# The head of a two-layer encoder trunk: first bias distances in the setup, two weight quarters in split form, the rope table behind the last split

## The chip, the cores and the metric

The kernel runs on one core of one Trainium2 chip. Its time is the device time in microseconds (us) of one execution, from first to last. Engines are named as the profile names them: PE is the matrix engine (TensorE) and PEld its weight loads, DVE is VectorE, ACT is ScalarE, POOL is GpSimd, SP is SyncE, which here only issues DMAs.

## The reference

The reference is a trunk of two layers over 256 tokens of width 2048, in float32. What matters for the change is the start of the first layer:

```
cond = silu(c)
for l in range(2):
    mod = cond @ w_ada[l] + b_ada[l]              # 2048 -> 6 * 2048
    sh_a, sc_a, g_a, sh_m, sc_m, g_m = split(mod, 6)
    h = rmsnorm(x) * (1 + sc_a) + sh_a
    proj = h @ w_in[l]                            # 2048 -> 3904 columns: dq, dk, dv, cq, ckv, kr
    ...  # differential attention with a bias by position distance,
    ...  # latent attention with rope on part of q and k
    x = x + g_a * (concat(out_a, out_b) @ w_o[l])
    h = rmsnorm(x) * (1 + sc_m) + sh_m
    x = x + g_m * (relu(h @ w_mlp_in[l])**2 @ w_mlp_out[l])
return rmsnorm(x, final_norm_g)
```

The bias of the differential attention is a table of 32 buckets by 4 heads, looked up by the bucket of the difference of two positions. Rope turns pairs of features by angles position times frequency, so it needs a table of cosines and sines.

## The kernel before, in words

Activations lie with features on the 128 partitions and the 256 tokens along the free dimension. The 2048 features are 16 k tiles, taken as eight pairs p = 0 to 7.

**Two forms of a weight.** A weight block is multiplied in one of two forms.

- Whole form: the float32 block is loaded straight into tiles of the tags `hi` and `lo` (`by_k_weights`, line 225) and multiplied with the float32 activation (line 244). One such product of 128 x 128 weights with 256 tokens shows up as two PE instructions in the trace.
- Split form: the block is loaded into a tile of the tag `raw` (line 156). ACT rounds each half of it into a `hi` tile (line 144), DVE takes the difference into a `lo` tile (line 145), and the product is three PE instructions (lines 180 to 182: hi times h's hi, hi times h's lo, lo times h's hi).

The tags `hi` and `lo` have four buffers each, and the tag `raw` has five, shared with the tiles of w_ada:

```
hi = self.wp.tile([P, half], F32R, tag="hi", name=self.name("hi"), bufs=4)
lo = self.wp.tile([P, half], F32R, tag="lo", name=self.name("lo"), bufs=4)
raw = self.wp.tile([P, width], F32, tag="raw", name=self.name("raw"), bufs=5)
```

**The head.** `setup` loads x, the condition and constants, and prepares the bias (`bias_setup`). `first_norm_then_by_k` then walks over the eight pairs. For each pair, four tiles of w_ada (1 MB each, `ada_load`, line 306) are multiplied with the condition and summed on DVE (`ada_sums`, line 322); this gives shift and scale of the pair's two k tiles (lines 334 and 336). DVE normalizes the pair (line 603), ACT applies scale and shift (line 614) and writes h's hi part (line 620), DVE writes h's lo part (line 626). PE multiplies the pair with the first 1536 columns (`w_a`, 12 tiles of 128 columns, two blocks). Pairs 0 to 5 (`WHOLE = 6`) are in whole form, pairs 6 and 7 in split form.

**What is filled in.** `FILL = "0|1|2|3||||rlm"` hangs small jobs behind the pairs: behind pairs 0 to 3 one part each of the bias, behind pair 7 the rope table (`rope_setup`), the lambdas and their end. A bias part needs distances (`bias_rel`: five DVE instructions, lines 472, 475 and 478), marks of the buckets (ACT line 489 and 494, DVE line 497) and 16 PE instructions (lines 507 and 508).

**The second columns.** `EARLY = {4: (0, 1), 6: (2,)}` names quarters of a second block of 512 columns (`w_d`, the rest of q and a part of k; a quarter is four k tiles, 1 MB). Quarters 0 and 1 are multiplied behind pair 4, quarter 2 behind pair 6, quarter 3 after the pairs. In the kernel before, quarters 0 to 2 are in whole form, since the float32 activations `whole` are there, and quarter 3 is in split form.

**Order.** The program is written in one sequence; a scheduler puts the instructions of each engine into an order of its own, by their place in the sequence and by when their data and buffers are there. `behind(a, b)` is a hint that a is issued after b on its engine. Each engine then runs its queue in order, and SP issues the DMAs in order.

Of the kernel before, what the change touches and what calls it, by code (L numbers as in the profile page):

```python
# [9 lines left out]
F32 = mybir.dt.float32  # L10
# [3 lines left out]
ALU = mybir.AluOpType  # L14
# [3 lines left out]
T = 256  # L18
# [40 lines left out]
def two_pi_parts():  # L59
    parts, rest = [], 2.0 * math.pi  # L60
    for _ in range(6):
        e = math.floor(math.log2(rest))
        q = 2.0 ** (e - 5)
        part = math.floor(rest / q) * q
        parts.append(part)
        rest -= part
    parts.append(rest)
    return parts
# [34 lines left out]
class Trunk:  # L103
# [31 lines left out]
    def weights(self, src, width=2048):  # L135
        nc = self.nc
        raw = self.raw(src, width)
        out = []
        half = width // 2
        for i in range(2):  # L140
            v = raw[:, i * half : (i + 1) * half]
            hi = self.wp.tile([P, half], F32R, tag="hi", name=self.name("hi"), bufs=4)
            lo = self.wp.tile([P, half], F32R, tag="lo", name=self.name("lo"), bufs=4)
            nc.scalar.activation(hi, v, AF.Copy)  # L144
            ins = nc.vector.tensor_tensor(lo, v, hi.bitcast(F32), ALU.subtract)  # L145
            out.append((hi, lo))
        self.ada_sums(self.hold or ins)
        self.credit += self.rate
        while self.credit >= 1.0 and self.ada_todo:
            self.credit -= 1.0  # L150
            self.ada_load()
        return out
# [200 lines left out]
    def setup(self):  # L353
        nc, io, cp = self.nc, self.io, self.cp
        self.ada_plan()
        self.cond = cp.tile([P, D], F32, name="cond")
        ck = cp.tile([P, NK], F32, name="ck")
        nc.sync.dma_start(ck, io["ck"])
        self.vec = cp.tile([P, NVEC], F32, name="vec")
        nc.sync.dma_start(self.vec, io["vec"])  # L360
        self.eps = cp.tile([P, 1], F32, name="eps")
        nc.gpsimd.memset(self.eps, EPS)
        self.K = cp.tile([P, NCONST], F32, name="K")
        nc.sync.dma_start(self.K, io["consts"])
        self.pos = cp.tile([P, T + 8], I32, name="pos")
        nc.sync.dma_start(self.pos, io["pos"])
        self.ones = cp.tile([P, P], F32, name="ones")
        nc.gpsimd.memset(self.ones, 1.0)
        self.ident = cp.tile([P, P], F32, name="ident")
        make_identity(nc, self.ident)  # L370
        xt = [[None, None], [None, None]]
        for h in range(2):
            for t in range(2):
                xt[t][h] = self.wp.tile([P, D // 2], F32, tag=("hi", "lo")[h], name=self.name("xt"), bufs=4)
                nc.sync.dma_start(xt[t][h], io["x"][t, :, D // 2 * h : D // 2 * h + D // 2])
        nc.scalar.activation(ck, ck, AF.Silu)
        nc.scalar.activation(self.s("root", 1), ck[:, :1], AF.Sqrt, bias=self.eps, scale=0.0)
        for j in range(4):
            c = slice(512 * j, 512 * j + 512)
            ps = self.bank("pc").rearrange("p a b -> p (a b)")  # L380
            for i in range(4):
                col = ck[:, 4 * j + i : 4 * j + i + 1].broadcast_to([P, P])
                nc.tensor.transpose(ps[:, i * P : i * P + P], col, self.ident)
            if j % 2:
                cond_dve = nc.vector.tensor_copy(self.cond[:, c], ps)
            else:
                cond_act = nc.scalar.activation(self.cond[:, c], ps, AF.Copy)
        self.bias_setup(cond_dve, cond_act)
        self.x = cp.tile([P, NK, T], F32, name="x")
        tot = self.sp.tile([P, 2, 2], F32, tag="s22", name="xsq")  # L390
        for h in range(2):
            for t in range(2):
                junk = self.bias[:, 2 * t : 2 * t + 2].rearrange("p a b c -> p (a b c)")
                ins = nc.scalar.activation(junk, xt[t][h], AF.Square, accum_out=tot[:, h, t : t + 1])
                self.behind(ins, cond_act)

        def turn(n, after=None):
            h, p = n // 4, n % 4
            ps = self.bank("px")
            for i in range(2):  # L400
                c = (2 * p + i) * P
                for t in range(2):
                    nc.tensor.transpose(ps[:, i, t * P : (t + 1) * P], xt[t][h][:, c : c + P], self.ident)
            k = 8 * h + 2 * p
            ins = nc.scalar.activation(self.x[:, k : k + 2], ps, AF.Copy)
            if after is not None:
                self.behind(ins, after)

        return tot, turn
# [108 lines left out]
    def rope_setup(self):  # L518
        nc, K, pos = self.nc, self.K, self.pos
        tl = lambda s: self.tp.tile([P, T], F32, tag="t", name=self.name(s))  # L520
        ang, k, r = tl("ang"), tl("kk"), tl("rr")
        self.behind(nc.vector.tensor_copy(ang, pos[:, :T]), self.last_mod)
        nc.vector.tensor_scalar(ang, ang, K[:, C_FREQ : C_FREQ + 1], None, ALU.mult)
        magic = 1.5 * 2.0**23
        nc.vector.tensor_scalar(k, ang, 1.0 / (2.0 * math.pi), magic, ALU.mult, ALU.add)
        nc.vector.tensor_scalar(k, k, -magic, None, ALU.add)
        src = ang
        for part in two_pi_parts():
            nc.vector.scalar_tensor_tensor(r, k, -part, src, ALU.mult, ALU.add)
            src = r  # L530
        pi = 3.1415925
        nc.vector.tensor_scalar(r, r, -pi, pi, ALU.max, ALU.min)
        self.cos = self.cp.tile([P, T], F32, name="cos")
        self.sin = self.cp.tile([P, T], F32, name="sin")
        c = tl("cc")
        nc.vector.tensor_scalar(c, r, -1.0, None, ALU.mult)
        nc.vector.tensor_tensor(c, c, r, ALU.max)
        nc.vector.tensor_scalar(c, c, -1.0, math.pi / 2.0, ALU.mult, ALU.add)
        nc.scalar.activation(self.sin, r, AF.Sin)
        nc.scalar.activation(self.cos, c, AF.Sin)  # L540
        nc.vector.tensor_scalar(self.sin, self.sin, K[:, C_SGN : C_SGN + 1], None, ALU.mult)
# [139 lines left out]
    def first_norm_then_by_k(self, acc, src, n, fill, early):  # L681
# [8 lines left out]
        ins = self.nc.scalar.activation(r, ps, AF.Copy)  # L690
# [3 lines left out]
        h, whole, made = [], [], []  # L694
# [14 lines left out]
        def first():  # L709

            nc = self.nc
            w = [[self.wp.tile([P, 6 * P], F32, tag=tag, name=self.name("w"), bufs=4) for tag in ("hi", "lo")]
                 for _ in range(2)]

            def load(i):
                self.ada_load()
                self.ada_load()
                for b in range(2):
                    nc.sync.dma_start(w[b][i], src[0, b, :, 6 * P * i : 6 * P * i + 6 * P])

            def second():
                load(1)
                self.ada_sums()

            load(0)
            self.ada_sums()
            self.behind(self.sums[0], sum_x)
            self.behind(self.sums[1], root)
            t = self.normed(r, 0, True)
            norm = self.last_norm  # L730
            new, lows, ins = self.scaled(t, 0, sh, sc, whole, second)
            self.rel = [self.bias_rel(a, norm) for a in range(2)]
            h.extend(new)
            made.append(ins)
            return lows, [(x, 6 * P) for x in w]

        lows, blocks = first()
        for p in range(8):
            if p:
# [33 lines left out]
    def layer(self, l, acc):  # L773
        nc, io = self.nc, self.io
# [5 lines left out]
        def next_by_k(kqs):  # L780
            def f(h, whole=()):
                if not later:
                    later.extend(self.open_banks(2))
                for kq in kqs:
                    f32 = whole if 4 * kq + 4 <= len(whole) else None
                    blocks = self.by_k_weights([io["w_d"][l, kq]], 4, f32)
                    self.by_k(later, blocks, h, 4 * kq, NK, 4, f32)
            return f
# [17 lines left out]
        kk, qn, kn, qr, vm, a, at, v, o = [], [], [], [], [], [], [], [], []  # L806
# [413 lines left out]
```

## Time and profile before

| | us |
|---|---|
| median of 3 runs | 2212.98 (2211.97 to 2214.62) |
| the profiled execution | 2212.55 |
| its span, first to last instruction | 2210.8 |
| PE busy | 2180.0 |
| DVE busy | 1625.5 |
| ACT busy | 1136.4 |
| bytes read | 581.28 MB, 264 GB/s over the span |

The busy time of PE is a share of the span, but matmuls are pipelined and their ends are modelled, so the pace of PE is better read from the starts of successive instructions. The head of the program, in which the change lies, is roughly the first 145 us of the span.

### The profile page before, as it was taken

To read this page: it belongs to the slowest core of one execution; us is meant where nothing else is said; L and a number is where in the kernel's file an instruction comes from. 1 tells how busy PE (TensorE), PEld (TensorE's weight loads), DVE (VectorE), ACT (ScalarE), POOL (GpSimd) and SP (SyncE) were. 2 spreads that over 40 slices of the span, in tenths; PEclk is the share of its full clock that TensorE was granted. 3 is DMA by queue.
4 is the path that set the end of the run, shared out by engine and by line. 5 is a ranking of instruction groups with operands and counts; after the bars stand their busy time and mean duration, and the time that the engine had idled before them with its cause. 6 is when DMAs were issued, how large, how long until landed. Compare 5 with 4: busy or idle time off the path is not lost.

```text
span 2210.8 us, 32403 instructions
## 1 busy us (share of the span) xinstructions
PE 2180.0 (99%) x13010; PEld 1948.1 (88%) x13010; DVE 1625.5 (74%) x2273; ACT 1136.4 (51%) x1691; POOL 1.9 (0%) x10
## 2 busy tenths in 40 slices
PE   7999999999999999999999999999999999999998
PEld 6899888998888888888889988988888888888887
DVE  7899779988878888887886876788655555555555
ACT  6555663465464355355444565546535534534553
POOL 0000000000000000000000000000000000000000
PEclk9999999999999999999999999999999999999999
DMA  9988778888878888888867666677655555555552
GB/s 379 415 348 311 265 269 327 316 328 325 322 305 321 305 323 310 318 324 304 316 218 265 248 229 228 236 263 253 240 189 193 184 189 192 188 183 192 188 189 95
DMA packets 85255, 585.49 MB, mean 265 GB/s; under 512 B 9584, under 2 KB 9968, under 8 KB 19440
## 3 DMA queue, kind: packets, MB, share of 16 engines
q1 hardware_dynamic: 85104, 583.42, 71.1%
q8 instruction: 102, 1.67, 0.3%
q14 instruction: 49, 0.40, 0.0%
HBM read 581.28 MB, written 2.10 MB: 264 GB/s over the span
## 4 chain that ended last, share of the span: by engine, by line
PE 93%; DVE 4%; DMA 2%; ACT 1%; issue 1%; SPq 0%; DVEq 0%; ACTq 0%
PE ps L201 43%; PE ps L204 22%; PE pk L244 3%; PE pk L182 2%; PE pk L181 2%; PE pk L180 2%; PE pk L258 2%; DVE ada L322 2%; PE pv L269 1%; PE pv L270 1%; PE pv L271 1%; DMA ada<-in_w_ada 1%; DVE lo L145 1%; PE pk L260 1%; PE ps L181 1%; PE ps L180 1%
## 5 line engine op out<-in xcount | busy, mean ns | idle before, releaser
L145 DVE TENSOR_TENSOR lo<-raw,hi 128x1024 fp32r<-128x1024 f32 (+1 forms) x714 | 843.0, 1194 | 466.9 <-issue 189.0
L144 ACT ACTIVATE hi<-raw 128x1024 fp32r<-128x1024 f32 (+1 forms) x714 | 731.3, 1035 | 690.6 <-PE ps L201 312.5
L201 PE MATMUL ps<-hid,hi 128*128 128x512 f32 x2048 | 477.5, 390 | 0.0
L322 DVE SCALAR_TENSOR_TENSOR ada<-ada,cond 128x2048 f32<-128x2048 f32 x192 | 438.6, 2286 | 13.6 <-DMA ada<-in_w_ada 13.5
L201 PEld LDWEIGHTS ps<-hid,hi 128*128 128x128 f32 x2048 | 379.7, 188 | 78.1 <-DVE hid L174 1.4
L201 PE MATMUL ps<-h,hi 128*128 128x512 f32 x1856 | 431.7, 390 | 0.0
L201 PEld LDWEIGHTS ps<-h,hi 128*128 128x128 f32 x1856 | 344.7, 188 | 69.2
L204 PEld LDWEIGHTS ps<-hid,lo 128*128 128x128 f32 x2048 | 254.2, 192 | 5.0
L204 PE MATMUL ps<-hid,lo 128*128 128x256 f32 x2048 | 255.7, 283 | 0.0
L204 PEld LDWEIGHTS ps<-h,lo 128*128 128x128 f32 x1856 | 230.3, 192 | 4.5
L204 PE MATMUL ps<-h,lo 128*128 128x256 f32 x1856 | 231.7, 283 | 0.0
L973 DVE SCALAR_TENSOR_TENSOR x<-ps,mod,x 128x256 f32<-128x256 f32 x272 | 124.6, 479 | 6.8 <-PE ps L204 6.6
L979 ACT ACTIVATE sum<-ps 128x256 f32<-128x256 f32 x110 | 42.2, 383 | 115.3 <-PE ps L204 115.1
L182 PE MATMUL pk<-h,lo 128*128 128x256 f32 x320 | 90.4, 283 | 0.0
L181 PE MATMUL pk<-h,hi 128*128 128x256 f32 x320 | 90.4, 283 | 0.0
L180 PE MATMUL pk<-h,hi 128*128 128x256 f32 x320 | 90.1, 285 | 0.0
L244 PE MATMUL pk<-hf,w 128*128 128x256 f32 x384 | 83.9, 379 | 0.0
L244 PEld LDWEIGHTS pk<-hf,w 128*128 128x128 f32 x384 | 72.6, 190 | 10.1 <-ACT hf L614 0.4
L174 DVE TENSOR_TENSOR hid<-relu,hid 128x256 fp32r<-128x256 f32 x128 | 48.3, 422 | 44.8 <-ACT hid L173 44.8
L182 PEld LDWEIGHTS pk<-h,lo 128*128 128x128 f32 x320 | 61.4, 192 | 0.2 <-DVE lo L145 0.2
L181 PEld LDWEIGHTS pk<-h,hi 128*128 128x128 f32 x320 | 61.4, 192 | 0.1
L180 PEld LDWEIGHTS pk<-h,hi 128*128 128x128 f32 x320 | 61.0, 192 | 0.1
(229 smaller groups left out, 2387.0 us busy)
## 6 DMA issues: line engine op xcount, KB each, us to landing
raw<-in_w_m SPq DMA_DIRECT2D x238, 1024.0 KB, 4.8
ada<-in_w_ada SPq DMA_DIRECT2D x192, 1024.0 KB, 4.9
raw<-in_w_ob SPq DMA_DIRECT2D x24, 1024.0 KB, 5.5
raw<-in_w_m SPq DMA_DIRECT2D x24, 768.0 KB, 5.7
raw<-in_w_dv SPq DMA_DIRECT2D x16, 1024.0 KB, 4.8
raw<-in_w_t SPq DMA_DIRECT2D x12, 1024.0 KB, 4.8
w<-in_w_a SPq DMA_DIRECT2D x24, 384.0 KB, 13.8
raw<-in_w_a SPq DMA_DIRECT2D x12, 768.0 KB, 5.4
```

Source lines behind the costliest of these rows:

```text
L144: nc.scalar.activation(hi, v, AF.Copy)
L145: ins = nc.vector.tensor_tensor(lo, v, hi.bitcast(F32), ALU.subtract)
L174: self.nc.vector.tensor_tensor(lo, val[:, i], hi.bitcast(F32), ALU.subtract)
L180: mm(ps, hi, x[0], start=first, stop=False, skip_group_check=shared)
L181: mm(ps, hi, x[1], start=False, stop=False, skip_group_check=shared)
L182: mm(ps, lo, x[0], start=False, stop=last, skip_group_check=shared)
L201: mm(ps.rearrange("p a b -> p (a b)"), part(w, k, 0), x[2], start=k == 0, stop=False)
L204: mm(ps[:, 0], part(w, k, 1), x[0], start=False, stop=k == nk - 1)
L244: self.nc.tensor.matmul(ps, v, whole[k], start=first, stop=last, skip_group_check=True)
L258: mm(ps.rearrange("p a b -> p (a b)"), part(j, 0), both, start=k == 0, stop=False)
L322: ins = nc.vector.scalar_tensor_tensor(w, w, 1.0, self.cond, ALU.mult, ALU.mult, accum_out=acc[:, i : i + 1])
L973: self.nc.vector.scalar_tensor_tensor(x, ps[i][:, j], g[:, m + i : m + i + 1], x, ALU.mult, ALU.add)
```

## The change

Three steps are changed.

- The distances of bias part 0 are computed at the end of `bias_setup`, where nothing orders them behind other work; before, `first` computed those of parts 0 and 1 behind the first normalization.
- Of the quarters of the second columns that are done early, only quarter 2 stays in whole form. Quarters 0 and 1 go to the split form: one DMA of 1 MB each into a `raw` tile, two roundings on ACT and two differences on DVE each, and 48 PE instructions in the place of 32.
- The first instruction of the rope table is ordered behind the last split (`last_lo`) that was written before it, which is that of pair 7; before, it was ordered behind the last shift and scale (`last_mod`).

```
@@ weights
-            ins = nc.vector.tensor_tensor(lo, v, hi.bitcast(F32), ALU.subtract)
+            ins = self.last_lo = nc.vector.tensor_tensor(lo, v, hi.bitcast(F32), ALU.subtract)
@@ setup
         self.bias_setup(cond_dve, cond_act)
+        self.rel = [self.bias_rel(0)]
@@ rope_setup
-        self.behind(nc.vector.tensor_copy(ang, pos[:, :T]), self.last_mod)
+        self.behind(nc.vector.tensor_copy(ang, pos[:, :T]), self.last_lo)
@@ first_norm_then_by_k, first
-            self.rel = [self.bias_rel(a, norm) for a in range(2)]
+            self.rel.append(self.bias_rel(1, norm))
@@ layer, next_by_k
-                    f32 = whole if 4 * kq + 4 <= len(whole) else None
+                    f32 = whole if kq == 2 else None
                     blocks = self.by_k_weights([io["w_d"][l, kq]], 4, f32)
                     self.by_k(later, blocks, h, 4 * kq, NK, 4, f32)
```

## The prediction

> **What bounds the kernel now.** I read the page first, then a table of stretches of 10 us over the head (four of them are shown), then the timelines of PE, DVE, ACT and SP around the three places of the change, then single DMAs with their time to landing. The page's head and its chain of waits:
>
> ```profile
> span 2210.8 us, 32403 instructions
> PE 93%; DVE 4%; DMA 2%; ACT 1%; issue 1%; SPq 0%; DVEq 0%; ACTq 0%
> ```
>
> The chain is PE almost to the end. So a shift of PE at the end of the head goes through to the end of the kernel. The head, by stretches (busy time of PE, PEld, DVE, ACT, POOL, then granted clock, DMA share, GB/s):
>
> ```profile
> 30.00:40.00 10.00, 6.70 (x25) 5.31 (x24) 9.96 (x13) 5.09 (x9) 0.00 (x0) 0.83 1.02 411
> 90.00:100.00 10.00, 10.00 (x48) 8.81 (x47) 6.01 (x8) 1.71 (x4) 0.00 (x0) 1.00 1.02 404
> 120.00:130.00 10.00, 10.00 (x76) 9.71 (x75) 9.86 (x14) 0.68 (x2) 0.00 (x0) 1.00 1.02 411
> 140.00:150.00 10.00, 10.00 (x87) 10.00 (x85) 7.99 (x9) 9.12 (x15) 0.00 (x0) 1.00 0.87 312
> ```
>
> From 90 to 130 us two things are full at once: PE without a gap, and the DMA queue (share 1.02, 404 to 411 GB/s, which is some 2.5 us for 1 MB). DVE and ACT have room from 90 to 100. In the stretch from 140 the DMA is no longer full.
>
> **Part 1, the first distances.**
>
> ```profile
> 13.29 0.16 DVE L688 TENSOR_TENSOR rms<-xsq 128x2 f32<-128x2 f32 x1 [1.97 <-ACT bias L394]
> 26.71 1.27 DVE L475 SCALAR_TENSOR_TENSOR rel<-fl,rt 128x256 f32<-128x256 f32 x3
> 27.90 0.42 DVE L478 TENSOR_SCALAR rel<-rel 128x512 f32<-128x512 f32 x1
> 43.41 2.29 DVE L322 SCALAR_TENSOR_TENSOR ada<-ada,cond 128x2048 f32<-128x2048 f32 x1 [2.14 <-DMA ada<-in_w_ada]
> ```
>
> Two of the three L475 (0.4 us each) and one L478 (0.42) leave the stretch at 27 us: 1.2 us of DVE there. DVE is back in step at 43.41, where it stands 2.14 us for a w_ada tile; that tile lands by a DMA queue that is full, so DVE being earlier before it buys nothing. In the setup the five instructions (about 1.9 us) lie in the wait of 1.97 us in front of 13.29. If that cover were gone, they would delay the root by up to 1.9 us, and the 2.14 us would swallow it. I take 0, with bounds of -0.3 and +0.3.
>
> **Part 2, the two quarters.** PE around the pairs 4 to 7:
>
> ```profile
> 70.31 10.52 PE L244 MATMUL pk<-hf,w 128*128 128x256 f32 x48
> 84.31 34.69 PE L244 MATMUL pk<-hf,w 128*128 128x256 f32 x160
> 118.65 0.70 PE L180 MATMUL pk<-h,hi 128*128 128x256 f32 x3
> 119.55 0.28 PE L181 MATMUL pk<-h,hi 128*128 128x256 f32 x1
> 119.67 0.28 PE L182 MATMUL pk<-h,lo 128*128 128x256 f32 x1
> 134.19 0.47 PE L180 MATMUL pk<-h,hi 128*128 128x256 f32 x1
> ...
> 134.77 0.39 PE L182 MATMUL pk<-h,lo 128*128 128x256 f32 x1
> 134.99 0.28 PE L180 MATMUL pk<-h,hi 128*128 128x256 f32 x1
> ```
>
> The 160 instructions are pair 4 (48), the two quarters (64) and pair 5 (48), at 34.69 / 160 = 0.217 us each. The split form starts one each 0.12 us. So the quarters take 64 x 0.217 = 13.9 us now and 96 x 0.12 = 11.5 us after: 2.35 us less PE.
>
> Against it stands when the first split is ready. PE is through with pair 4 at 84.31 + 48 x 0.217 = 94.7.
>
> ```profile
> 80.62 0.33 SPq L225 DMA_DIRECT2D w<-in_w_d  x1
> w<-in_w_d SPq DMA_DIRECT2D x1, 512.0 KB, 14.4
> L144 ACT ACTIVATE hi<-raw 128x1024 fp32r<-128x1024 f32 x642 | 671.5, 1057 | 616.0 <-PE ps L201 301.1 <-DMA raw<-in_w_m 87.2 <-DVE lo L145 81.6
> L145 DVE TENSOR_TENSOR lo<-raw,hi 128x1024 fp32r<-128x1024 f32 x642 | 774.9, 1220 | 454.8 <-issue 188.4 <-PE ps L204 172.6 <-ACT hi L144 93.5
> 95.02 1.09 ACT L614 ACTIVATE hf<-hf,mod,mod 128x256 f32<-128x256 f32 x2 [7.61 <-DVE mod L334]
> 96.02 0.71 ACT L620 ACTIVATE h<-hf 128x256 fp32r<-128x256 f32 x2
> 103.97 2.29 DVE L322 SCALAR_TENSOR_TENSOR ada<-ada,cond 128x2048 f32<-128x2048 f32 x1 [7.72 <-DMA ada<-in_w_ada]
> ```
>
> The second half of quarter 0 lands now at 80.62 + 14.4 = 95.0. As one DMA of 1 MB at the same place of a full queue, the quarter lands as a whole then. ACT's rounding takes 1.06 and DVE's difference 1.22. If ACT takes the rounding at once, the first split is ready at 95.0 + 1.06 + 1.22 = 97.3; behind the two L614 that become ready at the same moment (1.09) at 98.4; behind the two L620 also (0.71) at 99.1. PE starts two instructions of a product before it needs the lo tile (0.24). So PE stands 2.4, 3.4 or 4.1 us where it stood not at all. I take the middle, 3.4, since L614 comes earlier in the written sequence. The rest of the chain holds: half a quarter is 24 x 0.12 = 2.9 us of PE, and one rounding plus one difference is 2.3 us; DVE has its hole of 7.72 us in front of 103.97 for the four differences (4.9), ACT its idle stretch. Part 2 is then 3.4 - 2.35 = +1.05 us, with ends of 0 and +1.8.
>
> The standing itself may have a price of its own. At 33 us PE stood 3.3 us:
>
> ```profile
> 36.55 0.77 PE L507 MATMUL pb<-oh,lsch 128*128 128x512 f32 x1 [3.30 <-DVE oh L497]
> 37.11 0.63 PE L508 MATMUL pb<-oh,lscl 128*128 128x512 f32 x1
> 38.81 0.63 PE L508 MATMUL pb<-oh,lscl 128*128 128x512 f32 x1
> 40.00 0.40 PE L508 MATMUL pb<-oh,lscl 128*128 128x512 f32 x1
> 40.24 0.39 PE L507 MATMUL pb<-oh,lsch 128*128 128x512 f32 x1
> ```
>
> Behind it the starts are 1.70 / 4 = 0.43 us apart (37.11 to 38.81) instead of 0.24 (40.00 to 40.24); six of them lost some 1.2 us, and the stretch from 30 to 40 shows a clock of 0.83. [...]
>
> **Part 3, the rope table.** For pair 7 the starts 134.19 to 134.99 take 0.80 us for a product that takes 0.36 elsewhere: 0.44 lost.
>
> ```profile
> 129.21 0.29 DVE L522 CAST ang<-pos 128x256 f32<-128x256 int32 x1
> 131.58 2.26 DVE L529 SCALAR_TENSOR_TENSOR rr<-kk,rr 128x256 f32<-128x256 f32 x5
> 133.76 1.82 DVE L145 TENSOR_TENSOR lo<-raw,hi 128x768 fp32r<-128x768 f32 x2
> 138.46 1.04 ACT L144 ACTIVATE hi<-raw 128x1024 fp32r<-128x1024 f32 x1
> ```
>
> Rope starts at 129.21 on DVE, in front of pair 7's first difference at 133.76. With rope behind the differences the 0.44 us go. The price: rope's 15 steps on DVE, of 0.29 us (129.21) to 0.45 (five in 2.26), make 4.4 to 6.8 us, say 5.7, that now end later, and its sine and cosine on ACT may stand in front of quarter 3's rounding, at 138.46 now. PE needs that when it is through with pair 7's 24 products: 134.19 + 24 x 0.36 = 142.8. Pair 7's last difference can start when quarter 2 leaves PE at 134.19, and takes 0.9 (two in 1.82), so rope runs from 135.1 to 140.8; with sine and cosine in front (some 1.2 from the rows of ACT, as long as two L614) and then a rounding and a difference (2.3), PE would stand up to 1.5 us; if the rounding goes first, 0. I take +0.4, near the end at which the rounding goes first, since its data is there earlier. Part 3 is 0, between -0.4 and +1.
>
> **The sum.** 0 + 1.05 + 0 = +1.0 us on the profiled execution's 2212.55 (its span of 2210.8 and 1.75 around it), 2213.6. The median of the runs, 2212.98, is 0.43 higher, so the forecast for a median is 2214.0. This counts as no change: a measurement of this kernel can tell about 0.2%, which is 4.4 us.
>
> **The rivals.**
>
> *Held loads (slower).* Quarters 0 and 1 now fill eight hi and lo tiles instead of four, which is all there are.
>
> ```profile
> 87.09 8.10 SPq L225 DMA_DIRECT2D w<-in_w_a  x4
> 95.28 2.68 SPq L306 DMA_DIRECT2D ada<-in_w_ada  x4
> raw<-in_w_t SPq DMA_DIRECT2D x1, 1024.0 KB, 5.1
> 113.37 0.84 ACT L144 ACTIVATE hi<-raw 128x768 fp32r<-128x768 f32 x1 [16.64 <-issue]
> 115.99 0.75 DVE L626 TENSOR_TENSOR h<-hf,h 128x256 fp32r<-128x256 f32 x2
> ```
>
> Now pair 5's four loads leave from 87.09 to 95 as PE frees pair 4's tiles. If the quarters get these tiles first, pair 5's loads wait until PE is through with half of quarter 0: 98.1 + 2.9 = 101.0. SP issues in order, so the w_ada tiles of pair 6 (95.28) wait behind them. The queue runs dry when quarter 1 has landed (97.5) and moves again 5.1 - 2.5 = 2.6 us after the issue, at 103.6: a hole of 6.1 us in a queue that is full to 140. Pair 6's first raw tile, rounded at 113.37 now, comes at 119.5; from rounding to the pair's lo parts it is 3.4 us (113.37 to 116.74), so pair 6 starts near 122.9 instead of 118.65, +4.2, and the later loads, up to 6.1 late, add about 1: +5, 2218.0. It decides as soon as the hole is over 3 us. For it: tiles are short, and SP is in order. Against it: pair 5's loads need no data first, so they can be given the tiles that pair 3 freed by 70.31 + 10.4 = 80.7, before quarter 0 has landed; then they leave even earlier than now.
>
> *Clock halved behind the stand.* The forecast plus 1.2 us, 2215.2, if the stand is long enough.
>
> *No stand (faster).* If quarter 0 were loaded ahead of the last w_ada tile of pair 5, 2.5 us sooner, the stand is about 1 or none. Then 2.35 and 0.44 us come in, less what pair 6 asks back: PE would be there at 116.3, and its lo parts end at 116.74. That is -2.3 us, 2210.7. Against it: the written sequence puts the w_ada tiles first.
>
> *A difference behind a sum.* The last difference of quarter 1 is needed near 106.7. If DVE's order puts the sum of 103.97 (and the next) in front of it, it ends at 107.5 or 110: +0.8 to +3.3, 2214.8 to 2217.3. Then the change does only a part of what it says.
>
> **How the numbers follow.** Forecast 0.45; clock 0.15; held loads 0.22; no stand 0.10; difference behind a sum 0.08. Time: the forecast's 2214.0. The low end 2210.0 takes in "no stand" with 0.7 us of the spread of the runs; the high end 2218.5 takes in "held loads" at +5 with 0.5 for the clock. Outside lie held loads together with the halved clock, and an order of the later program that comes out otherwise. Slower by over 0.2% (above 2217.4): most of held loads, a part of the difference behind a sum, and the clock on top of either, 0.30. Faster by over 0.2% needs more than any term gives; I keep 0.10 for "no stand" with a better order behind it. Within: 0.60.
>
> **What would show it.** Right: 96 instructions of L180 to L182 between pair 4 and pair 5, 0.12 us apart, with PE waiting 2.4 to 4.1 us on L145 in front of them; pair 5's loads issued before 95; DMA share still 1.0 from 100 to 130; rope's first instruction behind pair 7's last L145 and no 0.44 us at pair 7. Held loads: a hole in the DMA share around 100 and pair 5's loads at 101 or later. Clock: starts 0.24 us apart and a granted clock under 1 behind the stand. The prediction is wrong if PE does not stand in front of the quarters, or if pair 7 starts more than 3 us from 135.

## The result and the profile after

The changed kernel takes 2216.4 us (median; 2213.8 to 2220.9), the kernel before, run beside it, took 2211.9 (2210.3 to 2216.4). The ratio is 1.002, with an interval of 1.0013 to 1.0027: slower by some 4.5 us, about the size of the 0.2% that the prediction called no change. The profiled execution took 2215.82 us against 2212.55, +3.3. Span and chain of waits on the page of the changed kernel:

```profile
span 2214.0 us, 32466 instructions
PE 88%; DVE 7%; DMA 4%; issue 1%; ACT 0%; SPq 0%; DVEq 0%; ACTq 0%
```

DVE and DMA have grown from 6% to 11% of the chain. The stretches (columns as above: busy time of five engines, granted clock, DMA share, GB/s) show where:

```profile
90.00:100.00 10.00, 6.68 (x34) 5.54 (x33) 8.34 (x12) 4.97 (x8) 0.00 (x0) 0.99 0.98 407
100.00:110.00 10.00, 10.00 (x74) 10.00 (x73) 6.92 (x8) 0.53 (x1) 0.00 (x0) 0.84 0.55 202
```

The second of them in the kernel before:

```profile
100.00:110.00 10.00, 10.00 (x49) 8.79 (x48) 5.81 (x6) 0.00 (x0) 0.00 (x0) 1.00 1.01 421
```

Two things are new. PE stands for 3.3 us between 90 and 100 and runs at a granted clock of 0.84 in the next 10 us. And in those same 10 us the DMA moves half of what it moved before (202 against 421 GB/s). The timeline of PE gives the first:

```profile
84.41 10.52 PE L244 MATMUL pk<-hf,w 128*128 128x256 f32 x48
97.73 0.39 PE L180 MATMUL pk<-h,hi 128*128 128x256 f32 x1 [2.80 <-ACT hi L144]
98.99 0.39 PE L182 MATMUL pk<-h,lo 128*128 128x256 f32 x1 [0.52 <-DVE lo L145]
100.23 0.42 PE L180 MATMUL pk<-h,hi 128*128 128x256 f32 x1
100.44 0.41 PE L181 MATMUL pk<-h,hi 128*128 128x256 f32 x1
100.66 0.41 PE L182 MATMUL pk<-h,lo 128*128 128x256 f32 x1
111.61 10.53 PE L244 MATMUL pk<-hf,w 128*128 128x256 f32 x48
121.78 0.47 PE L180 MATMUL pk<-h,hi 128*128 128x256 f32 x1
131.24 7.17 PE L244 MATMUL pk<-hf,w 128*128 128x256 f32 x32 [0.48 <-DMA w<-in_w_d]
146.89 0.28 PE L424 MATMUL pl<-vec,ones 128*128 128x4 f32 x2
```

Pair 4 ends at 94.93. The stand is 2.80 us at the first product and 0.52 at the first `lo`. Behind it instructions start 0.21 us apart (100.23, 100.44, 100.66) instead of 0.12. Pair 6, at 118.65 before, starts at 121.78: +3.1. The last row is the first product of the lambdas' sums. In the kernel before it is this one, 3.6 us earlier:

```profile
143.27 0.28 PE L423 MATMUL pl<-vec,ones 128*128 128x4 f32 x2
```

That row is the measure used from here on, "the sums". Behind it each kernel of this study needs another 2066.6 to 2069.7 us, so the sums leave up to 3 us of the whole time open. ACT and DVE around the stand:

```profile
95.03 1.09 ACT L615 ACTIVATE hf<-hf,mod,mod 128x256 f32<-128x256 f32 x2 [7.55 <-DVE mod L334]
96.02 0.71 ACT L621 ACTIVATE h<-hf 128x256 fp32r<-128x256 f32 x2
96.64 3.89 ACT L144 ACTIVATE hi<-raw 128x1024 fp32r<-128x1024 f32 x4
97.71 4.63 DVE L145 TENSOR_TENSOR lo<-raw,hi 128x1024 fp32r<-128x1024 f32 x4 [1.45 <-ACT hi L144]
112.68 2.29 DVE L322 SCALAR_TENSOR_TENSOR ada<-ada,cond 128x2048 f32<-128x2048 f32 x1 [5.72 <-DMA ada<-in_w_ada]
116.39 2.29 DVE L322 SCALAR_TENSOR_TENSOR ada<-ada,cond 128x2048 f32<-128x2048 f32 x1 [1.41 <-DMA ada<-in_w_ada]
```

ACT takes the roundings last, behind both pairs of activations. And DVE stands 5.72 us at 112.68 and 1.41 at 116.39 for w_ada tiles that pair 6 needs. Why they are late is in SP's queue (start, duration of the group, what it issues):

```profile
82.90 4.81 SPq L156 DMA_DIRECT2D raw<-in_w_d  x2
89.86 2.81 SPq L306 DMA_DIRECT2D ada<-in_w_ada  x2
102.81 3.92 SPq L225 DMA_DIRECT2D w<-in_w_a  x4
106.78 0.90 SPq L306 DMA_DIRECT2D ada<-in_w_ada  x2
```

Pair 5's four loads leave at 102.81, where they left at 87.09 before. They wait for `hi` and `lo` tiles, which the split quarters hold until PE is through with half of quarter 0 (its 24th instruction starts at 102.58); two w_ada tiles wait behind them in order.

### The profile page after: what moved, and what is told of

Same layout as the page of the kernel before. It is cut to its first block, busy times and chain, and to the rows that moved or that the text cites. A ratio compares the mean times of both kernels' runs of the same rounds, so it can differ in the third digit from the quotient of the medians.

```text
span 2214.0 us, 32466 instructions
## 1 busy us (share of the span) xinstructions
PE 2180.5 (98%) x13042; PEld 1950.1 (88%) x13042; DVE 1629.7 (74%) x2277; ACT 1140.0 (51%) x1695; POOL 1.9 (0%) x10
## 4 chain that ended last, share of the span: by engine, by line
PE 88%; DVE 7%; DMA 4%; issue 1%; ACT 0%; SPq 0%; DVEq 0%; ACTq 0%
PE ps L201 42%; PE ps L204 22%; DMA ada<-in_w_ada 3%; DVE ada L322 3%; PE pk L182 3%; PE pk L180 3%; PE pk L181 3%; DVE lo L145 2%; PE pk L258 2%; PE pv L269 1%; PE pv L270 1%; PE pv L271 1%; PE pk L260 1%; PE pk L244 1%; PE pw L600 1%
## 5 line engine op out<-in xcount | busy, mean ns | idle before, releaser
L180 PE MATMUL pk<-h,hi 128*128 128x256 f32 x352 | 100.2, 287 | 2.8 <-ACT hi L144 2.8
L182 PE MATMUL pk<-h,lo 128*128 128x256 f32 x352 | 100.0, 285 | 0.5 <-DVE lo L145 0.5
L181 PE MATMUL pk<-h,hi 128*128 128x256 f32 x352 | 100.1, 285 | 0.0
L180 PEld LDWEIGHTS pk<-h,hi 128*128 128x128 f32 x352 | 67.9, 194 | 3.3 <-ACT hi L144 3.2
L244 PE MATMUL pk<-hf,w 128*128 128x256 f32 x320 | 70.3, 379 | 0.5 <-DMA w<-in_w_d 0.5
L182 PEld LDWEIGHTS pk<-h,lo 128*128 128x128 f32 x352 | 68.3, 194 | 0.7 <-DVE lo L145 0.7
L244 PEld LDWEIGHTS pk<-hf,w 128*128 128x128 f32 x320 | 60.5, 190 | 9.0 <-DMA w<-in_w_d 0.7
L181 PEld LDWEIGHTS pk<-h,hi 128*128 128x128 f32 x352 | 68.3, 194 | 0.1
```

The costliest lines, as they stand in the source:

```text
L180: mm(ps, hi, x[0], start=first, stop=False, skip_group_check=shared)
L181: mm(ps, hi, x[1], start=False, stop=False, skip_group_check=shared)
L182: mm(ps, lo, x[0], start=False, stop=last, skip_group_check=shared)
L244: self.nc.tensor.matmul(ps, v, whole[k], start=first, stop=last, skip_group_check=True)
```

## The experiments

Three theories were to be told apart. A: PE's own loss, the stand and the slow stretch behind it, makes the time. B: the held loads make it, through a hole in a DMA queue that has no time to spare. C: the split form is dear wherever it lies. All thirteen kernels first; "pair 4" and "the sums" are the starts on PE in the profiled execution, GB/s is the mean of six stretches of 10 us from 80 to 140, ratios are against the kernel before, run beside each of them with medians of 2211.5 to 2212.1 us.

| kernel | ratio (interval) | pair 4 | the sums | GB/s 80-140 |
|---|---|---|---|---|
| before | 1 | 84.3 | 143.3 | 413 |
| the change | 1.002 (1.0013 to 1.0027) | 84.4 | 146.9 | 381 |
| split alone | 1.0023 (1.0013 to 1.0032) | 84.4 | 147.8 | 381 |
| distances and rope alone | 1.0007 (0.9999 to 1.0016) | 84.9 | 143.6 | 413 |
| rope alone | 1.0003 (0.9994 to 1.0012) | 83.8 | 142.5 | 417 |
| stand filled | 1.0021 (1.0012 to 1.003) | 83.9 | 146.1 | 388 |
| quarters loaded early | 1.0027 (1.0017 to 1.0036) | 85.8 | 148.0 | 376 |
| one quarter split | 1.001 (1.0001 to 1.0019) | 84.8 | 146.6 | 399 |
| whole, twice the buffers | 1.0028 (1.0017 to 1.0038) | 84.5 | 147.6 | 379 |
| split behind pair 5 | 1.001 (1.0001 to 1.0019) | 84.2 | 143.4 | 403 |
| whole behind pair 5 | 1.0021 (1.0012 to 1.003) | 84.5 | 145.5 | 402 |
| split, lows in raw ring | 1.0016 (1.0007 to 1.0025) | 85.7 | 145.2 | 392 |
| the same, loaded early | 1.0008 (0.9999 to 1.0017) | 84.6 | 144.9 | 398 |
| behind pair 5, raw ring | 1.0027 (1.0017 to 1.0037) | 84.3 | 148.1 | 371 |

By and large the last two columns go together: the fewer bytes are moved from 80 to 140, the later the sums. Between the change and before, 32 GB/s over 60 us are 1.9 MB, which take 4.6 us at 413 GB/s. That alone does not show which is the cause, since a late PE also frees tiles late and so holds loads back. And each profile is a single execution, from 2.4 us below (split, lows in raw ring) to 1.8 us above (behind pair 5, raw ring) the median of its kernel: a difference of a us at the sums needs the medians beside it.

**The parts of the change.** The split alone:

```
 (kernel before)
-    f32 = whole if 4 * kq + 4 <= len(whole) else None
+    f32 = whole if kq == 2 else None
```

> The kernel before with the second step alone: quarters 0 and 1 of the second columns in split form, distances and rope as before. Theory A (the loss is the quarters: PE stands from 94.9 until the first split is ready, and runs slowly behind the stand) and theory B (the loss is the loads of pair 5 and 6 that are held for tiles) both expect all of the loss here: pair 5 starts near 111.6 as in the changed kernel instead of 108.6, and the time is 3 to 5 us over the kernel before, with up to 0.5 more than in the changed kernel if the move of rope is worth something. A rival (the move of the distances or of rope costs the time) expects the time of the kernel before.

2217.26 us, ratio 1.0023: 5.7 us over the kernel before, a little more than the 3 to 5 expected. The loss is the split's. Its profile shows the same stand (3.11 us), the same slow products and the same hole as the whole change, and pair 5 at 111.54.

Distances and rope alone (the change with that line as it was):

> The changed kernel with quarters 0 and 1 back in whole form: first distances in the setup and rope behind pair 7's splits remain. Theories A and B expect the time of the kernel before, within 0.5 us, or up to 0.4 us less, since pair 7 then starts without the 0.44 us that its first product lost at 134.19. The rival that one of these two moves costs the time expects 2 to 4 us more than the kernel before.

2213.22 us, 1.6 us over the kernel before where at most 0.5 was expected, but with an interval that holds 1. The sums are 0.4 us later in a run whose pair 4 started 0.6 later.

The rope alone (kernel before):

```
-    self.behind(nc.vector.tensor_copy(ang, pos[:, :T]), self.last_mod)
+    self.behind(nc.vector.tensor_copy(ang, pos[:, :T]), self.last_lo)
```

> The kernel before with the rope's tables moved behind the last split and nothing else. By the prediction: 0.4 us gained at pair 7's first product, and at most as much lost behind it; the layer's sums start at 142.9 to 143.5 us (143.3 before), the time is 2211.2 to 2212.2 us. Rival, the rope moved is what makes up the 0.9 us by which the change with the split alone is later at the sums (147.8 us) than the whole change (146.9): then its place is worth 0.9 us here too, the sums start near 142.4 us and the time is 2211 us or under; and a second rival, that it costs: its sine falls among the roundings of quarter 3 or the first key block, the sums start at 143.6 us or later, as they do in the kernel with distances and rope moved.

2212.84 us, a little over the expected 2211.2 to 2212.2, and no difference that the interval shows. From pair 4 to the sums it is 58.7 us, in both runs with whole quarters and the rope moved, against 59.0 before: about 0.25 us gained in the head, where 0.44 were expected. The sums at 142.5 look like the first rival, but 0.5 us of that stood at pair 4 already, and the time did not follow. Of the 0.9 us between the split alone and the whole change the rope's place is only a part (see "Open" below).

**PE's stand, filled.** Twenty products of 128 x 128 between pair 4 and quarter 0, whose result is overwritten, keep PE busy where it stood:

```
 (the change; next_by_k, ahead of quarter 0)
+    if l == 0 and kq == 0:
+        for _ in range(20):
+            ins = nc.tensor.matmul(later[1][:, 1, :P], self.ident, whole[9][:, :P], start=True, stop=True, ...)
```

> The changed kernel, with 20 idle matmuls of 128 x 128 put on PE between pair 4 and quarter 0 (they write a bank that the quarter then starts anew), so that PE is busy while it waits for the first split. Theory A with its clock part: the products of quarter 0 start 0.36 us apart at once instead of 0.64 from 99.7 to 103.3, and pair 5 starts 1.6 us earlier, near 110.0. If the stand and the clock alone set the time, the kernel is 1.6 us faster than the changed one (about 2214.8 against 2216.4). Theory B: pair 6 has its data no earlier than about 121.6 (its lo parts in the changed kernel), so it starts within 0.3 us of 121.8 as before and the time is that of the changed kernel. If the slow stretch behind the stand is not due to the stand, the spacing of 0.64 us stays.

2216.31 us, as the change, where A alone expected 2214.8. PE's timeline and two of its stretches:

```profile
94.29 4.63 PE L790 MATMUL pk<-hf,ident 128*128 128x128 f32 x40
98.67 0.36 PE L180 MATMUL pk<-h,hi 128*128 128x256 f32 x1
98.87 0.28 PE L181 MATMUL pk<-h,hi 128*128 128x256 f32 x1
100.00:110.00 10.00, 10.00 (x85) 10.00 (x85) 6.68 (x7) 0.28 (x1) 0.00 (x0) 1.00 0.74 247
120.00:130.00 10.00, 9.42 (x76) 9.14 (x74) 9.96 (x12) 2.07 (x3) 0.00 (x0) 1.00 1.01 407
```

The clock is 1.00 from 100 to 110 and 85 instructions start there instead of 74, so the slow stretch is a consequence of the stand. Pair 5 starts at 110.27, as A expected (110.0), and pair 6 at 120.44, which is 1.1 us sooner than B allowed (121.5). One reason is that the two are linked: tiles come free as PE moves on, so pair 5's loads leave at 101.70 instead of 102.81. But the sums come only 0.8 us sooner: PE, earlier now, waits for data between 120 and 130 (1.0 us for quarter 2). A alone does not make the time.

**The stand taken away.** The raw loads of quarters 0 and 1 are issued ahead of pair 5's w_ada tiles:

```
 (the change; first_norm_then_by_k)
+    if p == 4:
+        self.ahead = [self.raw(self.io["w_d"][0, kq], 2048) for kq in (0, 1)]
     lows = ready(p + 1)
 (by_k_weights and weights then take these tiles instead of loading their own)
```

> The changed kernel, with the two 1 MB loads of quarters 0 and 1 issued ahead of the four w_ada tiles of pair 5 instead of behind them. Theory A alone: the first split is ready before 94.9, PE does not stand, the quarters take 11.5 us, pair 5 starts near 106.4 and everything behind comes 2.3 us earlier than in the kernel before: about 2209.6. Theory B: pair 5's four loads still wait for tiles that quarter 0 holds until PE is through with its halves (97.8 and 100.7), the DMA queue has a hole of 2 to 3 us, pair 6 gets its data at 119 instead of 116.7, and the time is within 1 us of the kernel before (2211 to 2213).

2217.44 us: no stand ahead of quarter 0, and not faster. Both theories missed the time, A (2209.6) and B (2211 to 2213, which priced the hole too low). Pair 4 started 1.4 us late in this profile, behind stretches from 30 to 50 us with a clock of 0.82 and 0.84, which explains little of it. SP and the stretch:

```profile
76.09 16.09 SPq L306 DMA_DIRECT2D ada<-in_w_ada  x4
99.08 3.68 SPq L225 DMA_DIRECT2D w<-in_w_a  x4
90.00:100.00 10.00, 10.00 (x63) 9.25 (x62) 10.00 (x10) 2.39 (x3) 0.00 (x0) 1.00 0.58 224
```

Pair 5's loads still leave only at 99.08, and the hole has moved to 90 to 100. PE goes through the two quarters and pair 5 and then stands 3.3 us ahead of pair 6, for pair 6's `h`. The stand was moved, not removed.

**The held tiles by themselves.** Whole quarters, each in four tiles of half the size, so that they take as many buffers as the split form, with no split, no rounding and no stand:

```
 (distances and rope moved, quarters whole; by_k_weights, cut = 2 for quarters 0 and 1)
+    half //= cut
-    w = [self.wp.tile([P, half], F32, tag=tag, ...) for tag in ("hi", "lo")]
+    w = [self.wp.tile([P, half], F32, tag=tag, ...) for tag in ("hi", "lo") * cut]
```

> The kernel with distances and rope moved and whole quarters, but each of quarters 0 and 1 in four half-size tiles instead of two, so that it takes as many buffers as the split form does, with no split, no rounding and no stand. Held loads: pair 5's loads wait for quarter 0's tiles, which come free one by one from 97 to 102 us; they are issued there instead of from 87.1 us, the DMA share of 90 to 100 us falls to 0.5 to 0.8, pair 6 gets its data 2 to 5 us later than 119.3 us, the layer's sums start at 145 to 148 us (143.6 with the same quarters in two tiles) and the time is 2214.5 to 2218 us. Rival, the buffers are of no account and the split's own stand and slow products made the loss: the sums start within 0.7 us of 143.6 us and the time is 2211.5 to 2213.5 us.

2217.75 us, ratio 1.0028. SP, a stretch and PE:

```profile
79.33 16.06 SPq L226 DMA_DIRECT2D w<-in_w_d  x8
96.79 5.51 SPq L226 DMA_DIRECT2D w<-in_w_a  x4
90.00:100.00 10.00, 10.00 (x48) 8.81 (x47) 5.66 (x8) 1.70 (x4) 0.00 (x0) 1.00 0.78 259
131.97 7.17 PE L245 MATMUL pk<-hf,w 128*128 128x256 f32 x32 [2.70 <-DMA w<-in_w_d]
147.60 0.28 PE L425 MATMUL pl<-vec,ones 128*128 128x4 f32 x2
```

The kernel to compare with is distances and rope alone. It does the same work with the same data in fewer buffers: here the sums come 4.0 us later (147.6 against 143.6) and the median is 2217.75 us against 2213.22. The loads are also smaller (256 KB each instead of 512), but the DMA moved 420 GB/s from 80 to 90 us, as with the larger ones (423), so the size is not what it lost by. Holding the tiles alone is dear enough for the whole loss. The place was not the expected one, though. Pair 6 was only 0.6 us late (119.85 against 119.27), where 2 to 5 were expected. The bytes that the queue had not moved in the hole were a debt, and it fell due at quarter 2, with a wait of 2.70 us.

**One quarter split** (the change with `f32 = whole if whole and kq in (0, 2) else None`):

> The changed kernel with only quarter 1 of the second columns in split form; quarter 0 is whole again. PE's work falls by 32 x 0.217 - 48 x 0.12 = 1.2 us against whole quarters. Held loads: quarter 1's roundings lie under quarter 0's products, so PE does not stand between pair 4 and quarter 0; one raw load instead of two goes ahead of pair 5's loads, so these are held less than in the changed kernel (issued there from 102.8 us on), and the DMA share of 100 to 110 us is over 0.8 instead of 0.55. The layer's sums (the products with the ones, at 143.3 us before, 146.9 us with the change, 143.6 us with whole quarters, distances and rope moved) then start at 142.5 to 144.5 us and the time is 2211 to 2213.5 us. Rival, the split form is dear by itself at this place, by half for one quarter: the sums start at 145.2 us, half way, and the time is 2214 us or more.

2214.1 us. The loads are held less (92.75), the DMA share of 100 to 110 is 0.84, and pair 6 starts at 118.42, sooner than before. But then:

```profile
129.29 8.86 PE L244 MATMUL pk<-hf,w 128*128 128x256 f32 x32 [1.88 <-DMA w<-in_w_d]
130.00:132.00 2.00, 2.00 (x6) 1.55 (x6) 1.34 (x3) 0.59 (x2) 0.00 (x0) 0.50 1.03 430
```

Quarter 2 waits 1.88 us for its loads and then runs at half the clock for a while (8.86 us instead of 7.07). The sums, at 146.6, missed the 142.5 to 144.5 that B expected, and the time is over B's 2213.5 as well. By both numbers the run falls on the side of its rival, that the split form is dear by itself (145.2, 2214 or more), though the time does so by 0.1 us. The trace names other causes: the wait is for loads, and the slow stretch, which B had not counted, cost 1.8 us. So this run does not decide between B and C.

**Another place.** Quarters 0 and 1 behind pair 5, where the raw loads can be queued behind pair 5's own:

```
 (the change)
-EARLY = {4: (0, 1), 6: (2,)}
+EARLY = {5: (0, 1), 6: (2,)}
+    if p == 5:
+        self.ahead = [self.raw(self.io["w_d"][0, kq], 2048) for kq in (0, 1)]
```

> The changed kernel with quarters 0 and 1 (split) computed behind pair 5 instead of pair 4, their raw loads issued behind pair 5's own loads and ahead of pair 6's modulation weights. Held loads: nothing is queued ahead of pair 5's loads any more, so they are issued near 80 us, the DMA share stays over 0.95 from 80 to 120 us, PE does not stand for roundings, and the 2.4 us of PE's work that the split saves come out whole or in part: the layer's sums start at 141 to 143.3 us (146.9 with the change, 143.3 before), the time is 2209 to 2212 us. Rival, the split form is dear by itself (its roundings on ScalarE and VectorE keep these from the modulation and make pair 6 late, wherever the quarters lie): the sums start at 145 us or later, the time is 2214 us or more.

The same place with whole quarters:

> The kernel with distances and rope moved and all quarters whole, quarters 0 and 1 computed behind pair 5 instead of pair 4: the place of the run with the split quarters behind pair 5, without the split. If the place alone costs nothing (held loads: no load is queued ahead of pair 5's), the layer's sums start at 143 to 144 us, the time is 2211 to 2213.5 us, and the split kernel of the same place is 1 to 2.4 us ahead of it. Rival, the place itself gains or costs (PE stands ahead of pair 5, whose data now come right behind pair 4 at 99.6 us instead of under the quarters): PE waits up to 5 us at pair 5's first product, which is given back at pair 6 if pair 6's data come at 118.6 us as before.

2213.51 us split, 2216.41 whole. Neither is as fast as expected (up to 2212 and 2213.5), and the split kernel's sums, at 143.43, are just behind the expected 143.3; its rival had them at 145 or later. At this place the split form is 2.9 us faster than the whole one; the sums are 2.1 us apart (143.43 and 145.50), 1.8 if counted from pair 4 on. PE's waits of 0.3 us and more from pair 4 to the sums add up to the same 1.8 us in both, so the difference is PE's work. So C falls: the 2.35 us of PE are real, and most of them come out where the quarters do not hold up pair 5's loads. The place costs about as much:

```profile
95.57 10.63 PE L244 MATMUL pk<-hf,w 128*128 128x256 f32 x48 [0.83 <-ACT hf L615]
106.29 1.23 DVE L145 TENSOR_TENSOR lo<-raw,hi 128x1024 fp32r<-128x1024 f32 x1 [2.70 <-PE pk L244]
118.24 0.62 PE L180 MATMUL pk<-h,hi 128*128 128x256 f32 x3 [0.55 <-ACT h L621]
143.43 0.28 PE L424 MATMUL pl<-vec,ones 128*128 128x4 f32 x2
```

PE waits 0.83 us for pair 5's activation and 0.55 at pair 6 (and 0.42 at its second instructions), and DVE stands 2.70 us at a `lo` tile that pair 5's products still hold, with four w_ada sums behind it that then run without a wait for their tiles. Again it is the tiles.

**Tiles from the other ring.** The `hi` parts of the two quarters take one `hi` and one `lo` tile each, as whole quarters do, and the `lo` parts one tile each of the raw ring:

```
 (weights, for quarters 0 and 1)
+    los = self.wp.tile([P, width], F32R, tag="raw", ..., bufs=5)
-    hi = self.wp.tile([P, half], F32R, tag="hi", ...)
-    lo = self.wp.tile([P, half], F32R, tag="lo", ...)
+    hi = self.wp.tile([P, half], F32R, tag=("hi", "lo")[i], ...)
+    lo = los[:, i * half : (i + 1) * half]
```

First the change with it, then with the raw loads early as well, then behind pair 5:

> The changed kernel with the split parts of quarters 0 and 1 in other buffers: their high parts take one tile of each of the two four-buffer rings, as whole quarters do, and their low parts one tile each of the five-buffer ring of raw tiles, which the modulation weights share. Held loads: pair 5's loads no longer wait for quarter 0; they are issued from 85 to 98 us instead of 102.8 to 106.7, and the DMA share of 100 to 110 us rises from 0.55 to over 0.8. ScalarE's order is as in the change, so TensorE still stands about 3 us ahead of quarter 0. If the loads decide alone, the layer's sums start at 143 to 145 us (146.9 with the change) and the time is 2211 to 2214 us. If stand and slow clock decide too (theory that both come at the same moment), pair 6 still starts within 1 us of 121.8 and the time is 2214.5 to 2216.5 us. Third, the held tiles of the raw ring hold the modulation weights or pair 6's raw loads instead: the hole moves behind 105 us, and the sums start at 146 us or later.

> The kernel of the last experiment with the raw loads of quarters 0 and 1 issued ahead of pair 5's modulation weights as well, so that their rounding is done under pair 4. If stand and held loads together are the whole cost, TensorE goes from pair 4 to quarter 0 without a wait, pair 5's loads are issued before 98 us, pair 6 starts at 116.5 to 118.5 us, the layer's sums start at 141 to 143.3 us and the time is 2209.5 to 2212 us. If the buffers are the matter and it doesn't help from which ring they come, the five-buffer ring now holds the modulation weights of pair 5 or 6: the DMA share falls under 0.8 in a stretch of 10 us between 85 and 115 us, pair 6 waits for its data, and the time is 2214 us or more.

> The split quarters behind pair 5 with their raw loads early, as in the earlier run of that place, and their low parts in tiles of the raw ring as in the two runs after it. In that earlier run VectorE stood 2.7 us at 106.29 us, in quarter 1's last subtraction, which waited for a buffer that pair 5's products still held; four modulation weights had landed behind it, and TensorE then waited 0.8 us at pair 5 and 0.9 us at pair 6. If those waits are all that keeps the saved 2.4 us from coming out, the subtraction no longer waits, TensorE's waits for pair 6 vanish, the layer's sums start at 141.5 to 142.6 us (143.4 in the earlier run) and the time is 2211 to 2212.5 us, that of the kernel before or under it. If the DMA queue, with a share of 1.0 from 20 us on, decides, the waits move to pair 6's data or to quarter 2's loads, the sums start at 143 to 145 us and the time is 2213 to 2215 us: the split quarters gain nothing wherever they lie.

2216.33, 2213.95 and 2217.69 us. SP, a stretch and PE of the first; a stretch of the second; SP and a stretch of the third:

```profile
90.67 5.89 SPq L226 DMA_DIRECT2D w<-in_w_a  x4
100.00:110.00 10.00, 10.00 (x85) 10.00 (x85) 7.75 (x9) 0.92 (x1) 0.00 (x0) 1.00 0.85 325
98.12 0.39 PE L181 MATMUL pk<-h,hi 128*128 128x256 f32 x1 [1.92 <-ACT hi L145]
```

```profile
100.00:110.00 10.00, 9.78 (x75) 9.37 (x74) 8.24 (x11) 1.71 (x4) 0.00 (x0) 1.00 0.98 352
```

```profile
89.47 16.56 SPq L307 DMA_DIRECT2D ada<-in_w_ada  x4
110.00:120.00 10.00, 10.00 (x73) 10.00 (x73) 10.00 (x14) 3.18 (x6) 0.00 (x0) 0.83 0.57 184
```

In the first, pair 5's loads leave at 90.67, the hole is 0.85 instead of 0.55, and the sums come 1.7 us sooner than with the change. The profile does not separate the hold from the clock here, as pair 4 started 1.3 us late and so the stand was only 1.92 us, without a slow stretch behind it. And the median shows nothing of it: 2216.33 is what was expected if stand and slow clock decide too (2214.5 to 2216.5). The second has no wait over 0.5 us at the quarters and no slow clock there. It is the best version with both quarters split in the old place, but the sums, at 144.9, are still 1.6 us behind the kernel before, and 1.6 behind the upper end of what was expected: quarter 2 waits 1.45 us for its loads. In the third the raw ring holds the w_ada tiles (four issues stretch over 16.56 us) and the hole is back, at 110 to 120, with 0.57. It answers to neither expectation; it is the second theory of the run before it, that the ring from which the tiles come makes no difference.

Four of the kernels form a table of their own. Over the kernel before, the change has 1.0020, the early loads alone 1.0027, the other ring alone 1.0016, and both together 1.0008. Each step by itself gains nothing clear of the noise; with both, 2213.95 us, more than half of the loss is gone. None of the twelve beats the kernel before.

## Why the prediction was right or wrong

The forecast of 2214.0 was 2.4 us low, and the time is inside the range. As a difference the miss is larger: +1.0 was forecast and +4.5 measured, since the kernel before, run beside the changed one, came out 1.1 us lower than the 2212.98 that the forecast starts from. By its own signs the forecast's mechanism failed: pair 5's loads did not leave before 95, the DMA share was not 1.0 from 100 to 130, and pair 7 started at 138.07, 3.1 us from 135, where more than 3 was to mean wrong. The step that failed is the one on the tiles, "held loads" below. That the time still lies inside is partly luck: held loads and halved clock came together, which the text had put outside the range, but their prices overlap instead of adding up. By its steps:

**Part 1, 0: borne out.** In the trace after, DVE stands 2.84 us (2.14 before) at the same w_ada tile:

```profile
43.42 2.29 DVE L322 SCALAR_TENSOR_TENSOR ada<-ada,cond 128x2048 f32<-128x2048 f32 x1 [2.84 <-DMA ada<-in_w_ada]
```

It starts at 43.42 against 43.41. What DVE gained it waits out there, as the step said. In the setup the distances lie in the wait ahead of the root, which starts at 12.91 (13.29 before).

**Part 2, the saving: right.** Behind the slow stretch the products start 0.12 us apart (0.36 each), and at the place where nothing holds pair 5's loads the split gives about 1.8 us of the 2.35 at the sums.

**Part 2, the stand: the order was the wrong one of three.** The text took 3.4 us, with the roundings behind L614; ACT put them behind L620 too, the case of 4.1. The first product with `lo` started at 98.99, where that case has the split ready at 99.1. PE's waits were 2.80 + 0.52 = 3.3 us, with some 0.4 more in pauses between the first nine instructions (97.73 to 99.69, 1.96 us, less nine at 0.12 and the 0.52).

**Part 2, the clock: the rival came in.** From 99.7 to 103.3 us a product takes 0.64 us instead of 0.36; that is 5.6 products and 1.6 us, where the rival said 1.2. For its condition, a stand that is long enough, the text shows one case, the 3.30 us at 33 us; no run shows a length that decides (the stands are in the last section). Stand, saving and slow stretch explain pair 5 at 111.61, which is 3.0 us late (before, 84.31 + 112 x 0.217 = 108.6): 3.3 + 0.4 for the pauses + 1.6 - 2.35 = 2.95.

**Part 2, the held loads: the step that failed.** The forecast took the side "they leave even earlier than now", so the sum has nothing for them; they left at 102.81, where the rival said 101.0. The tiles that pair 3 freed went to the quarters, and SP's wait for them ended with PE's L182, the quarter's own products. The rival's chain is confirmed link by link: the hole in 100 to 110, w_ada behind it, pair 6's first raw tile rounded at 118.20 (rival 119.5, before 113.37). Its price of +4.2 at pair 6 was +3.1, and with the debt at quarter 2 (0.48 us) the sums came 3.6 us late. The two causes do not add up: pair 6's data and PE, each some 3 us late, meet at 121.6 to 121.8. That is why taking away the slow stretch, or the stand, gained nothing by itself. The held tiles alone cost as much as the change, but by another road: there the debt fell due at quarter 2.

**Part 3, 0: borne out, with both terms smaller.** Rope starts behind pair 7's last difference, and pair 7's first product takes 0.55 us (138.07 to 138.62) where it took 0.80:

```profile
138.07 0.47 PE L180 MATMUL pk<-h,hi 128*128 128x256 f32 x1
138.62 0.28 PE L180 MATMUL pk<-h,hi 128*128 128x256 f32 x1
136.05 3.57 DVE L145 TENSOR_TENSOR lo<-raw,hi 128x768 fp32r<-128x768 f32 x4 [0.28 <-ACT hi L144]
139.53 0.29 DVE L523 CAST ang<-pos 128x256 f32<-128x256 int32 x1
```

The gain is 0.25 us and not 0.44. The other 0.19 were never the rope's: the first product of pair 6 takes 0.55 us too (121.78 to 122.33), with no rope near. The price was misread as well. The sum took 1.2 us of ACT for sine and cosine; their rows in the kernel before show 0.42 each and a table load of 1.28 ahead of them. The sine came at 147.18, behind the roundings of quarter 3, so PE did not pay there. A price shows up further on, in PE's waits:

```profile
PE psm L1103 <- DVE sm L1105: 2.2, 2, 1.7
```

The columns are us in total, times and longest. It is 0.5 us in one wait in the two kernels with the rope in its old place, and 2.2 or 2.3 in all others. What leads to it was not followed; the total of the rope alone shows no difference.

**Open.** 0.9 us at the sums lie between the split alone and the whole change. Up to pair 6 the two are level (121.72 and 121.78). Then quarter 2 waits 0.99 us for its loads in the split alone against 0.48, and pair 7's first product takes 1.00 us there against 0.55. The second half is the rope's place; why the loads of quarter 2 came later was not followed. The distances alone were not run, and no version was found in which the split quarters gain.

## What to carry to other kernels

A form that saves time on the matrix engine may take more buffers, and in a stretch where the DMA queue is full the buffers are the prefetch (here, with eight tiles held instead of four, the DMA moved 202 instead of 421 GB/s from 100 to 110 us): price them by which load now waits for which product, and by the bytes that the queue then does not move. With two limits full at once, relieving one gives at most what the other has to spare (with the stand filled pair 6 started 1.3 us sooner, the sums 0.8); look for the debt at the next load without slack, which need not be the next in line. Two causes that make the same thing late by about the same time must both be taken away before anything is gained, so a test that removes one and finds nothing does not clear it (1.0027 with the early loads alone, 1.0016 with the other ring alone, 1.0008 with both).

## What the runs showed of the hardware

The clock behind a stand does not follow the length of the stand alone. Behind stands of PE of 2.80 (the change), 3.11 (split alone), 3.30 (quarters loaded early), 3.11 (behind pair 5, raw ring) and 1.88 us (one quarter split) it fell. The granted clock reads 0.50 from 100 to 103 us in the change and from 130 to 132 us with one quarter split. In the other three its means over 10 us are 0.92 and 0.91 (90 to 110), 0.83 (120 to 130) and 0.83 (110 to 120), and instructions of the split form start 0.21 us apart behind the stand instead of 0.12, as in the change. Behind 2.70 us (whole, twice the buffers) and 1.92 us (split, lows in raw ring) it stayed at 1.00. What the five slow stretches have in common is their length. Added up from the granted clock of stretches of 10 us, each is 3.4 to 3.6 us at half the clock (3.42 by stretches of 1 us in the change), which cost 1.6 us in the change and 1.8 us with one quarter split. At 33 us PE stands 2.5 to 4.2 us in every kernel (what its busy time leaves of 30 to 40 us). The slow stretch behind it, added up in the same way from 30 to 50 us, is 3.4 us long in six of the fourteen and 6.8 us, twice that, in the other eight.

```profile
132.00:134.00 2.00, 2.00 (x9) 1.78 (x10) 1.13 (x3) 0.80 (x2) 0.00 (x0) 1.00 1.02 420
```

These are the 2 us behind the stand of 2.70 us. The runs show neither what sets the length of a slow stretch nor why 1.88 us of standing was enough in one kernel and 2.70 us was not in another.
